# Values as the stationary operand in three attention mixers, two heads side by side in the columns of the array

## The chip, the cores and the metric

The kernel runs on one core of a Trainium2 chip. The metric is the device time of one execution in microseconds (us). The core's engines are TensorE (PE in the rows, and PEld for its weight loads), VectorE (DVE), ScalarE (ACT), GpSimd (POOL) and SyncE (SP), and DMA queues move data. PE works at one of two clocks, 1.2 or 2.4 GHz; the profile states the granted clock of a stretch as a share of 2.4 GHz.

## What is computed

Two stacks of two layers on 512 tokens of 1024 features, all in float32. A layer of block 1 mixes tokens in three ways (mLSTM, HGRN2, sliding-window attention with sinks) and then has an MLP and a gated embedding. A layer of block 2 mixes with differential, dilated and forgetting attention and then has a gated MLP with a convolution. The three attentions that the change touches, cut to what matters:

```python
# window attention (block 1): 8 query heads on 2 key/value heads of 64, window 128
m = jnp.maximum(jnp.max(s, axis=-1, keepdims=True), sink)
pexp = jnp.exp(s - m)
probs = pexp / (jnp.sum(pexp, axis=-1, keepdims=True) + jnp.exp(sink - m))
o = jnp.einsum('bnhgqk,bnkhd->bnqhgd', probs.astype(v.dtype), vv)

# forgetting attention (block 2): 6 heads of 64, causal
s = jnp.einsum('bhqd,bhkd->bhqk', qblk, k).astype(jnp.float32) * scale
s = s + fq[..., :, None] - cum_logf[..., None, :]
s = jnp.where(kpos[None, :] <= qpos[:, None], s, -jnp.inf)
p = jax.nn.softmax(s, axis=-1)
return jnp.einsum('bhqk,bhkd->bhqd', p, vf)

# dilated attention (block 2): 6 heads of 64, a mixture of windowed patterns,
# which the kernel computes as one softmax with an additive table c_dil
```

## The kernel before

**Numbers.** A large product is made of three (`mm3`, L176 to L178): each operand is split into a high and a low part (`split`, L136 on ACT and L137 on DVE), and high x high, high x low and low x high are summed in PSUM. These "triple products" are the projections. The attentions' own products (scores, transposes, product with the values) are plain float32, each of scores and values in two records.

**Tiles.** 512 tokens are four token tiles of 128 (`NT = 4`). Names of tiles: `ysw`, `yc`, `yb`, `ya` hold values and outputs by token (128 tokens in the partitions); `slotA` and `slotB` hold feature-major data; `wh` and `wl` are split weights, which `wload` brings ahead (`wr`, three buffers).

**PSUM.** `ps(tag)` takes a tile from one of four rings: "mm" with three buffers, "S" and "T" with two each, "o" with one. Buffers of a ring go round in the order of the program. Projections take "mm" (inside `held` also "S" and "T"), scores take "S", transposes "T", and the output of an attention tile is "o".

**Window attention** (`swa`). First a preparation: squares and sums of the heads (L534, L535), a reciprocal root (`rsqrt`, L121 to L132), the rotation (L548 to L559), and 20 transposes into feature-major queries and keys (L564). Then for each token tile and each of 8 heads: score (L581), masked maximum (L583, L584), exponential with its sum (L585), transposes (L590); after two heads a copy to `sw_pT` (L593) and the product with the values (L597), with the transposed probabilities as the stationary operand and 64 columns of values moving. At the end of a token tile all eight heads are scaled by the reciprocal sums in one DVE instruction (L603). Behind it in the program stand `feat(0)`, `feat(1)` and the `w_hi1` projection.

**Forgetting attention** (in `mixers2`, L1149 on). Gates: four transposes (L1136), steps on 6 x 512 (L1141 to L1147), a DMA to DRAM (`fg_d`) and, for each head and token tile, a DMA that broadcasts it to all partitions (`fg_b`, L1157, issued by POOL). Then `softmax_block` (score L1093, causal mask by a product L1096, DVE L1099, exponential L1100) and `pv` (transposes L1109, copy L1111, product with the values L1113). Token tiles go from the last to the first; L1162 scales. Behind it in the program stand the projections of differential attention (`w_a2`, through `rope_proj`; its steps L1068 to L1071, L1085, L1086).

**Dilated attention** (`attend`, L1219 on) is built in the same way with the table `c_dil`, token tiles 0 to 3, in two halves. After each half its output is transposed (L1251), split and projected (`w_ob2`); behind the first half stand also the projections `w_oa2`.

**Order.** Nothing here is ordered by hand. The program states the work mixer by mixer; a scheduler at build time moves instructions of later parts ahead where their operands and buffers are free by the program's own order of rings. So projections that stand behind a mixer can run between its steps. `tick` and `start` (L216 to L240) let the steps of the next normalization advance with the work of PE.

Of the kernel before, what the change touches and what calls it, by code (L numbers as in the profile page):

```python
# [9 lines left out]
F32 = mybir.dt.float32  # L10
F32R = mybir.dt.float32r
# [3 lines left out]
ALU = mybir.AluOpType  # L15
# [4 lines left out]
P = 128  # L20
S = 512
NT = S // P
# [39 lines left out]
class Builder:  # L62
# [328 lines left out]
    def mixers1(self, l, mp, act, nxt):  # L391
        nc = self.nc
        X, Y = self.sets
# [34 lines left out]
        ysw = [mp.tile([P, 768], F32, name=f"ysw{t}") for t in range(NT)]  # L428
# [16 lines left out]
        w = self.wload("w_hi1", l, 8 * 256)  # L445
# [8 lines left out]
        w = self.wload("w_mv1", l, 8 * 264, parts=4)  # L454
# [42 lines left out]
        sink = lambda m, pt, sl: nc.vector.tensor_tensor(self.x[m][:, sl], self.x[m][:, sl], pt, ALU.add)  # L497
        act = [self.to_feat(X, sub(ysw, i), "mm") for i in range(4)]
        for g in range(2):
# [23 lines left out]
    def swa(self, l, mp, sp, ysw, row):  # L523
# [44 lines left out]
        for t in range(NT):  # L568
# [9 lines left out]
            for j in range(8):  # L578
# [524 lines left out]
    def pv(self, mp, s, t, po, v):  # L1103
# [8 lines left out]
        for c in range(t + 1):  # L1112
            nc.tensor.matmul(po, pT[:, c * P:c * P + P], v(c), start=c == 0, stop=c == t)  # L1113

    def mixers2(self, l, mp, act, nxt):
        nc = self.nc
# [34 lines left out]
        for t in reversed(range(NT)):  # L1151
            po = self.ps("o")
            den = mp.tile([P, 6], F32, name="at_den", tag="at_den", bufs=2)
            for h in range(6):
                fbt = mp.tile([P, S], F32, name="fg_b", tag="fg_b", bufs=3)
                w = (t + 1) * P
                nc.gpsimd.dma_start(fbt[:, :w], fd[0, h * S:h * S + w].partition_broadcast(P))  # L1157
                b = (h % 2) * 64
                s, dn = self.softmax_block(mp, qk[h // 2][b:b + 64], qk[3 + h // 2][b:b + 64], t, fbt[:, :w], 0.125, True)
                nc.vector.reciprocal(den[:, h:h + 1], dn)  # L1160
                self.pv(mp, s, t, po[:, h * 64:h * 64 + 64], lambda c: yc[c][:, h * 64:h * 64 + 64])
            nc.vector.tensor_tensor(yc[t][:, 0:384].rearrange("p (h e) -> p h e", e=64),  # L1162
                                    po[:, 0:384].rearrange("p (h e) -> p h e", e=64),
                                    den.unsqueeze(2).broadcast_to([P, 6, 64]), ALU.mult)

# [50 lines left out]
        sub = lambda y, i: [y[t][:, i * P:i * P + P] for t in range(NT)]  # L1216
        act = [self.to_feat(X, sub(yc, i)) for i in range(3)] + [self.to_feat(X, sub(ya, i)) for i in range(2)]

        def attend(t):  # L1219
            po = self.ps("o")  # L1220
            den = mp.tile([P, 6], F32, name="at_den", tag="at_den", bufs=2)
            for h in range(6):
                b = (h % 2) * 64
                s, dn = self.softmax_block(mp, qkb[h // 2][b:b + 64], qkb[3 + h // 2][b:b + 64], t,
                                           self.c_dil[:, (3 - t) * P:], 0.125)
                nc.vector.reciprocal(den[:, h:h + 1], dn)
                self.pv(mp, s, t, po[:, h * 64:h * 64 + 64], lambda c: yb[c][:, h * 64:h * 64 + 64])
                self.tick(3000)
            nc.vector.tensor_tensor(yo[t].rearrange("p (h e) -> p h e", e=64),
                                    po[:, 0:384].rearrange("p (h e) -> p h e", e=64),  # L1230
                                    den.unsqueeze(2).broadcast_to([P, 6, 64]), ALU.mult)

# [6 lines left out]
        for sl in HALVES:  # L1239
# [3 lines left out]
            if wo is None:  # L1243
# [277 lines left out]
```

## Time and profile before

| | |
|---|---|
| median of 3 runs | 2808.39 us (2804.37 to 2814.62) |
| the profiled execution | 2820.27 us |
| its span | 2818.4 us |
| mean granted clock | 0.984 |
| PE busy | 2749.6 us, 98% |
| DVE, ACT, POOL busy | 63%, 42%, 8% |

The profiled execution stands 0.4% above the median. A row of the timeline gives the start, the busy time, engine, line and operation of consecutive equal instructions, then the tiles, partitions x elements, and a count; in brackets stands the idle time of the engine just before, with what ended it. Records of PE overlap each other, so what one costs is read from the distance between starts, not from its duration.

### The profile page before, as it was taken

To read this page: it belongs to the slowest core of one execution; us is meant where nothing else is said; L and a number is where in the kernel's file an instruction comes from. 1 tells how busy PE (TensorE), PEld (TensorE's weight loads), DVE (VectorE), ACT (ScalarE), POOL (GpSimd) and SP (SyncE) were. 2 spreads that over 40 slices of the span, in tenths; PEclk is the share of its full clock that TensorE was granted. 3 is DMA by queue.
4 is the path that set the end of the run, shared out by engine and by line. 5 is a ranking of instruction groups with operands and counts; after the bars stand their busy time and mean duration, and the time that the engine had idled before them with its cause. 6 is when DMAs were issued, how large, how long until landed. Compare 5 with 4: busy or idle time off the path is not lost.

```text
span 2818.4 us, 42688 instructions
## 1 busy us (share of the span) xinstructions
PE 2749.6 (98%) x16408; PEld 2350.0 (83%) x16408; DVE 1778.9 (63%) x3842; ACT 1176.3 (42%) x2296; POOL 214.2 (8%) x558
## 2 busy tenths in 40 slices
PE   8999999999999999999999999999999999999998
PEld 7887887889978788788987888888889787988887
DVE  7677777468767857756844656655554375665555
ACT  4644532236374553232634445433234444442332
POOL 2000100002200010000212100000000210000000
PEclk9998999999999999999999999999999999999999
DMA  4211486332221128733223121223332312133222
GB/s 153 75 50 50 141 266 222 105 103 92 85 70 46 61 93 265 254 120 105 91 75 111 31 70 64 84 88 96 100 106 77 87 36 86 39 105 98 90 88 77
DMA packets 87645, 285.61 MB, mean 101 GB/s; under 512 B 10972, under 2 KB 15132, under 8 KB 87440
## 3 DMA queue, kind: packets, MB, share of 16 engines
q1 hardware_dynamic: 81280, 266.49, 29.5%
q0 software_dynamic: 5872, 16.35, 2.3%
q8 instruction: 129, 2.11, 0.3%
q14 instruction: 76, 0.62, 0.1%
q10 hardware_dynamic: 288, 0.03, 0.0%
HBM read 280.69 MB, written 2.14 MB: 100 GB/s over the span
## 4 chain that ended last, share of the span: by engine, by line
PE 78%; DVE 8%; DMA 7%; ACT 2%; POOL 2%; issue 2%; SPq 0%; DVEq 0%; POOLq 0%; ACTq 0%
PE ps_mm L176 12%; PE ps_mm L177 12%; PE ps_mm L178 12%; DMA wm<-w_mod 6%; PE ps_T L176 5%; PE ps_T L177 5%; PE ps_T L178 5%; PE ps_S L176 5%; PE ps_S L177 5%; PE ps_S L178 5%; PE ps_S L1093 3%; PE ps_o L1113 2%; DVE wm L1032 2%; PE ps_T L1109 1%; PE ps_S L581 1%
## 5 line engine op out<-in xcount | busy, mean ns | idle before, releaser
L136 ACT CAST wh<-wr 128x1024 fp32r<-128x1024 f32 (+4 forms) x414 | 407.2, 986 | 672.5 <-PE ps_mm L177 209.3
L137 DVE TENSOR_TENSOR wl<-wr,wh 128x1024 fp32r<-128x1024 f32 (+4 forms) x414 | 476.0, 1151 | 317.4 <-ACT wh L136 309.9
L177 PE MATMUL ps_mm<-slotA,wh 128*128 128x512 f32 (+1 forms) x632 | 229.0, 364 | 3.4 <-DVE slotA L317 2.0
L176 PE MATMUL ps_mm<-slotA,wh 128*128 128x512 f32 (+1 forms) x632 | 226.5, 365 | 1.5 <-ACT slotA L316 0.7
L178 PE MATMUL ps_mm<-slotA,wl 128*128 128x512 f32 (+1 forms) x632 | 226.3, 360 | 0.0
L176 PE MATMUL ps_mm<-wh,slotA 128*128 128x256 f32 (+3 forms) x688 | 208.7, 304 | 1.3 <-DVE rp_b L1070 1.3
L178 PE MATMUL ps_mm<-wh,slotA 128*128 128x256 f32 (+3 forms) x688 | 206.1, 300 | 0.0
L177 PE MATMUL ps_mm<-wl,slotA 128*128 128x256 f32 (+3 forms) x688 | 205.7, 299 | 0.0
L1032 DVE CUSTOM_DVE_ANT_0 wm<-wm,sc 128x1024 f32<-128x1024 f32 x96 | 117.5, 1224 | 65.9 <-DMA wm<-w_mod 65.2
L136 ACT CAST m_h<-tmp 128x512 fp32r<-128x512 f32 (+1 forms) x122 | 71.4, 587 | 207.6 <-DVE tmp L911 171.3
L176 PE MATMUL ps_mm<-slotB,wh 128*128 128x512 f32 (+1 forms) x408 | 141.9, 357 | 2.6 <-ACT slotB L136 1.6
L177 PE MATMUL ps_mm<-slotB,wh 128*128 128x512 f32 (+1 forms) x408 | 142.5, 351 | 1.4 <-DVE slotB L137 1.4
L176 PEld LDWEIGHTS ps_mm<-wh,slotA 128*128 128x128 f32 x688 | 131.4, 191 | 13.7 <-issue 12.2
L177 PEld LDWEIGHTS ps_mm<-slotA,wh 128*128 128x128 f32 x632 | 122.3, 194 | 22.7 <-issue 3.1
L178 PE MATMUL ps_mm<-slotB,wl 128*128 128x512 f32 (+1 forms) x408 | 140.7, 346 | 0.0
L176 PEld LDWEIGHTS ps_mm<-slotA,wh 128*128 128x128 f32 x632 | 121.4, 194 | 22.7 <-issue 3.6
L178 PEld LDWEIGHTS ps_mm<-slotA,wl 128*128 128x128 f32 x632 | 122.3, 193 | 17.5 <-issue 2.6
L178 PEld LDWEIGHTS ps_mm<-wh,slotA 128*128 128x128 f32 x688 | 131.4, 191 | 6.2 <-issue 5.1
L177 PEld LDWEIGHTS ps_mm<-wl,slotA 128*128 128x128 f32 x688 | 131.5, 191 | 5.8 <-issue 5.0
L176 PE MATMUL ps_S<-m_h,wh 128*128 128x512 f32 (+1 forms) x355 | 129.5, 365 | 2.4 <-DVE yacc L945 2.1
L1100 ACT ACTIVATE at_s<-at_s,at_st 128x512 f32<-128x512 f32 (+3 forms) x160 | 89.6, 560 | 98.3 <-DVE at_st L1099 91.2
L178 PE MATMUL ps_S<-m_h,wl 128*128 128x512 f32 (+1 forms) x355 | 129.3, 364 | 0.0
(631 smaller groups left out, 7289.9 us busy)
## 6 DMA issues: line engine op xcount, KB each, us to landing
wr<-w_up SPq DMA_DIRECT2D x152, 512.0 KB, 3.8
wm<-w_mod SPq DMA_DIRECT2D x96, 512.0 KB, 4.6
wr<-w_dn SPq DMA_DIRECT2D x64, 512.0 KB, 3.9
wr<-w_dn SPq DMA_DIRECT2D x32, 384.0 KB, 3.0
wr<-w_dn SPq DMA_DIRECT2D x32, 320.0 KB, 2.8
wr<-w_f SPq DMA_DIRECT2D x16, 512.0 KB, 3.8
wr<-w_pg SPq DMA_DIRECT2D x16, 512.0 KB, 3.8
wr<-w_t SPq DMA_DIRECT2D x12, 512.0 KB, 4.7
```

The lines of the kernel that those rows point to most:

```text
L136: nc.scalar.copy(hi, src)
L137: nc.vector.tensor_tensor(lo, src, hi.bitcast(F32), ALU.subtract)
L176: nc.tensor.matmul(out, ah, bh, start=i == 0, stop=False)
L177: nc.tensor.matmul(out, ah, bl, start=False, stop=False)
L178: nc.tensor.matmul(out, al, bh, start=False, stop=i == n - 1)
L581: nc.tensor.matmul(pt, qs[f][b:b + 64, tt], qs[4][b:b + 64, k0:k0 + w], start=True, stop=True)
L1032: nc.vector.tensor_tensor_reduce(w, w, self.sc, 1.0, 0.0, ALU.mult, ALU.add, accum_out=self.mod[l][:, j:j + 1])
L1093: nc.tensor.matmul(pt, q[:, t * P:w], k[:, 0:w], start=True, stop=not tri, tile_position=None if row is None else (row, 0))
L1100: nc.scalar.activation(s, s, AF.Exp, bias=st[:, 0:1], scale=-1.0, accum_out=st[:, 1:2])
L1109: nc.tensor.transpose(tp[:, c * P:c * P + P], s[:, c * P:c * P + P], self.ident)
L1113: nc.tensor.matmul(po, pT[:, c * P:c * P + P], v(c), start=c == 0, stop=c == t)
```

## The change

In the three mixers the product with the values is turned round. The values (128 tokens x 64 features of one head) are the stationary operand, the transposed probabilities (128 queries) move, and two heads go to the two column halves of the array by `tile_position` (0,0) and (0,64). The output has features in the partitions: two heads in 128 rows, queries along the columns. To scale it, `out_scaled` needs the reciprocal sums in the same layout: POOL spreads them over 64 columns a head, PE transposes them into a PSUM tile of the ring "mm", ACT copies them, and DVE multiplies. Outputs are now feature-major, so `to_feat` and the transposes at the end of dilated attention give way to `parts_of` and plain splits. In forgetting and dilated attention two heads now go together through `pv2`. Differential attention keeps `pv`.

```diff
-        act = [self.to_feat(X, sub(ysw, i), "mm") for i in range(4)]
+        act = [self.parts_of(X, ysw, i) for i in range(4)]
...
-                    for jj in (j - 1, j):
-                        for c in range(w // P):
-                            o, v = (jj % 2) * w + c * P, 640 + (jj % 2) * 64
-                            nc.tensor.matmul(po[:, jj * 64:jj * 64 + 64], pT[:, o:o + P], ysw[k0 // P + c][:, v:v + 64],
-                                             start=c == 0, stop=c == w // P - 1)
+                    for c in range(w // P):
+                        for u in range(2):
+                            o, v = u * w + c * P, 640 + u * 64
+                            nc.tensor.matmul(po[u * 64:u * 64 + 64, f * P:f * P + P], ysw[k0 // P + c][:, v:v + 64],
+                                             pT[:, o:o + P], start=c == 0, stop=c == w // P - 1, tile_position=(0, u * 64))
...
-            nc.vector.tensor_tensor(ysw[t][:, 0:512].rearrange("p (h e) -> p h e", e=64),
-                                    po.rearrange("p (h e) -> p h e", e=64),
-                                    den.unsqueeze(2).broadcast_to([P, 8, 64]), ALU.mult)
+            self.out_scaled(ysw[t][:, 0:512], po, den, 4)
...
+    def pv2(self, mp, ss, t, po, v):
...
+        w = (t + 1) * P
+        pTs = []
+        for s in ss:
+            tp = self.ps("T")
+            for c in range(t + 1):
+                nc.tensor.transpose(tp[:, c * P:c * P + P], s[:, c * P:c * P + P], self.ident)
+            pT = mp.tile([P, S], F32, name="at_pT", tag="at_pT", bufs=3)[:, :w]
+            nc.scalar.copy(pT, tp[:, :w])
+            pTs.append(pT)
+        for c in range(t + 1):
+            for u, pT in enumerate(pTs):
+                nc.tensor.matmul(po[u * 64:u * 64 + 64], v(c, u), pT[:, c * P:c * P + P], start=c == 0, stop=c == t,
+                                 tile_position=(0, u * 64))
+
+    def out_scaled(self, dst, po, rden, n):
...
+        pr = self.ps("mm")
+        rb = self.tmp()[:, 0:n * P]
+        nc.gpsimd.tensor_copy(rb.rearrange("p (h e) -> p h e", e=64), rden.unsqueeze(2).broadcast_to([P, 2 * n, 64]))
+        for i in range(n):
+            nc.tensor.transpose(pr[:, i * P:i * P + P], rb[:, i * P:i * P + P], self.ident)
+        nc.scalar.copy(rb, pr[:, 0:n * P])
+        nc.vector.tensor_tensor(dst, po[:, 0:n * P], rb, ALU.mult)
+
+    def parts_of(self, which, ys, i):
...
+        h, lo = self.slot(which, F32R), self.slot(which, F32R)
+        for t in range(NT):
+            tt = slice(t * P, t * P + P)
+            self.split(h[:, tt], lo[:, tt], ys[t][:, i * P:i * P + P])
+        return h, lo
...
-            for h in range(6):
...
-                nc.vector.reciprocal(den[:, h:h + 1], dn)
-                self.pv(mp, s, t, po[:, h * 64:h * 64 + 64], lambda c: yb[c][:, h * 64:h * 64 + 64])
-                self.tick(3000)
...
+            for i in range(3):
...
+                self.pv2(mp, ss, t, po[:, i * P:i * P + P], lambda c, u: yb[c][:, (2 * i + u) * 64:(2 * i + u) * 64 + 64])
+                self.tick(6000)
+            self.out_scaled(yo[t], po, den, 3)
...
-            for i in range(3):
-                pt = self.ps("T")[:, 0:S // 2]
-                for u, t in enumerate(ts):
-                    nc.tensor.transpose(pt[:, u * P:u * P + P], yo[t][:, i * P:i * P + P], self.ident)
-                self.split(aa[i][0][:, sl], aa[i][1][:, sl], pt)
+            for t in ts:
+                tt = slice(t * P, t * P + P)
+                for i in range(3):
+                    self.split(aa[i][0][:, tt], aa[i][1][:, tt], yo[t][:, i * P:i * P + P])
```

The order of instructions moves with it. First PE in window attention of the first layer, where its first token tile ends and the second begins, before the change. L176 to L178 are triple products, L581 scores, L590 transposes, L597 products with the values:

```order
L177 MATMUL ps_mm_1612<-wl_1551,slotA_114 128x264
L597 MATMUL ps_o_770<-ysw0_205,sw_pT_824 128x64 x2
L581 MATMUL ps_S_879<-sw_q4_765,slotB_744 128x256
L178 MATMUL ps_mm_1612<-wh_1550,slotA_115 128x264
L590 MATMUL ps_T_862<-ident_81,sw_s_858 128x128 x2
L176 MATMUL ps_mm_1612<-wh_1550,slotA_116 128x264
L581 MATMUL ps_S_888<-sw_q4_765,slotB_744 128x256
L177 MATMUL ps_mm_1612<-wl_1551,slotA_116 128x264
L178 MATMUL ps_mm_1612<-wh_1550,slotA_117 128x264
L176 MATMUL ps_mm_1640<-wh_1532,slotA_102 128x264
L177 MATMUL ps_mm_1640<-wl_1533,slotA_102 128x264
L597 MATMUL ps_o_770<-ysw0_205,sw_pT_843 128x64 x2
```

The same engine and place after the change; L1137 are the transposes of `out_scaled`:

```order
L581 MATMUL ps_S_864<-sw_q4_765,slotB_737 128x256
L597 MATMUL ps_o_770<-sw_pT_805,ysw0_205 64x128 x2
L581 MATMUL ps_S_873<-sw_q4_765,slotB_737 128x256
L590 MATMUL ps_T_834<-ident_81,sw_s_830 128x128
L597 MATMUL ps_o_770<-sw_pT_824,ysw0_205 64x128 x2
L590 MATMUL ps_T_834<-ident_81,sw_s_838 128x128
L581 MATMUL ps_S_887<-sw_q4_765,slotB_744 128x256
L590 MATMUL ps_T_870<-ident_81,sw_s_866 128x128 x2
L581 MATMUL ps_S_896<-sw_q4_765,slotB_744 128x256
L597 MATMUL ps_o_770<-sw_pT_843,ysw0_205 64x128 x2
L1137 MATMUL ps_mm_851<-ident_81,tmp_852 128x128 x4
L590 MATMUL ps_T_870<-ident_81,sw_s_875 128x128 x2
```

Between the steps of the attention stood triple products of the projections before; now the steps follow each other without any.

The second place is PE at the end of forgetting attention in the first layer of block 2, before the change. L1109 are transposes, L1113 products with the values, L1093 and L1096 score and mask:

```order
L177 MATMUL ps_mm_15444<-wl_15383,slotA_13680 128x256
L178 MATMUL ps_mm_15444<-wh_15382,slotA_13681 128x256
L176 MATMUL ps_mm_15444<-wh_15382,slotA_13682 128x256
L177 MATMUL ps_mm_15444<-wl_15383,slotA_13682 128x256
L1113 MATMUL ps_o_14878<-yc0_14482,at_pT_14961 128x64
L1113 MATMUL ps_o_14878<-yc1_14483,at_pT_14961 128x64
L1109 MATMUL ps_T_14995<-ident_81,at_s_14990 128x128
L1093 MATMUL ps_S_15032<-slotB_14067,slotB_14064 128x128
L1096 LDWEIGHTS identb_14052
L1096 MATMUL ps_S_15032<-trib_14054,identb_14052 128x128
L1093 MATMUL ps_S_15047<-slotB_14068,slotB_14065 128x128
L1113 MATMUL ps_o_14878<-yc0_14482,at_pT_14978 128x64
```

And after it, where L1121 are the transposes of `pv2` and L1127 its products with the values:

```order
L1127 MATMUL ps_o_15076<-at_pT_15100,yc0_14554 64x128
L1127 MATMUL ps_o_15076<-at_pT_15104,yc0_14554 64x128
L1127 MATMUL ps_o_15076<-at_pT_15130,yc0_14554 64x128
L1121 MATMUL ps_T_15158<-ident_81,at_s_15143 128x128
L1127 MATMUL ps_o_15076<-at_pT_15134,yc0_14554 64x128
L1127 MATMUL ps_o_15076<-at_pT_15160,yc0_14554 64x128
L1121 MATMUL ps_T_15162<-ident_81,at_s_15153 128x128
L1127 MATMUL ps_o_15076<-at_pT_15164,yc0_14554 64x128
L1137 MATMUL ps_mm_15168<-ident_81,tmp_15169 128x128 x3
L176 MATMUL ps_mm_15192<-wh_15182,slotA_13752 128x256
L177 MATMUL ps_mm_15192<-wl_15183,slotA_13752 128x256
L178 MATMUL ps_mm_15192<-wh_15182,slotA_13753 128x256
```

The first triple product of the projections for differential attention, on `ps_mm_15192`, now stands behind the last transposes of `out_scaled` (L1137); before, triple products stood between the steps.

## Rows read from the trace of the kernel before

**Rows 1.** The page, part 1: busy us, share of the span, instructions.

```profile
PE 2749.6 (98%) x16408; PEld 2350.0 (83%) x16408; DVE 1778.9 (63%) x3842; ACT 1176.3 (42%) x2296; POOL 214.2 (8%) x558
```

**Rows 2.** The page, part 4: the chain that ended last, by engine.

```profile
PE 78%; DVE 8%; DMA 7%; ACT 2%; POOL 2%; issue 2%; SPq 0%; DVEq 0%; POOLq 0%; ACTq 0%
```

**Rows 3.** Windows: from:to, length, busy us of engines, granted clock, DMA share, GB/s.

```profile
78.30:166.50 88.20, 88.20 (x554) 70.67 (x552) 52.22 (x170) 50.77 (x117) 1.07 (x2) 1.00 0.22 70
...
1505.60:1572.00 66.40, 65.99 (x439) 52.60 (x440) 25.23 (x94) 33.03 (x86) 14.21 (x25) 0.95 0.30 74
...
1507.50:1514.20 6.70, 6.70 (x22) 4.63 (x23) 2.29 (x10) 4.17 (x10) 2.35 (x4) 0.51 0.51 142
1705.50:1712.10 6.60, 6.60 (x20) 3.79 (x19) 1.98 (x8) 2.10 (x7) 0.00 (x0) 0.51 0.06 25
...
1514.40:1572.00 57.60, 57.60 (x414) 47.38 (x414) 21.93 (x79) 27.82 (x74) 11.31 (x20) 1.00 0.27 64
```

**Rows 4.** Timeline of PE at 2.4 GHz in forgetting attention.

```profile
1515.77 1.12 PE L1093 MATMUL ps_S<-slotB 64*128 64x512 f32 x2
1516.83 2.00 PE L1113 MATMUL ps_o<-yc,at_pT 128*128 128x64 f32 x16
1518.66 1.04 PE L1109 MATMUL ps_T<-ident,at_s 128*128 128x128 f32 x8
1519.54 0.22 PE L1096 MATMUL ps_S<-trib,identb 128*128 128x128 bf16 x1
```

**Rows 5.** Timeline of PE: scores between triple products of 256 columns, window attention.

```profile
85.81 0.28 PE L176 MATMUL ps_mm<-wh,slotA 128*128 128x256 f32 x1
85.93 0.28 PE L177 MATMUL ps_mm<-wl,slotA 128*128 128x256 f32 x1
86.14 0.48 PE L581 MATMUL ps_S<-sw_q,sw_q 64*128 64x128 f32 x2
86.55 0.39 PE L178 MATMUL ps_mm<-wh,slotA 128*128 128x256 f32 x1
86.77 0.28 PE L176 MATMUL ps_mm<-wh,slotA 128*128 128x256 f32 x1
```

**Rows 6.** Timeline of PE: records of one 64x64 tile.

```profile
871.53 1.14 PE L729 MATMUL ps_S<-tmp 64*64 64x64 f32 x16
872.61 0.44 PE L590 MATMUL ps_T<-ident,sw_s 128*128 128x128 f32 x2
```

**Rows 7.** Timeline of PE: records that alternate between two column halves.

```profile
911.15 1.91 PE L733 MATMUL ps_S<-tmp 64*64 64x64 f32 x64
912.99 0.39 PE L177 MATMUL ps_mm<-wl,slotB 128*128 128x256 f32 x1
```

**Rows 8.** Timeline of PE: the first steps of forgetting attention.

```profile
1505.71 1.12 PE L1093 MATMUL ps_S<-slotB 64*128 64x512 f32 x2 [2.73 <-DVE at_st L1099]
...
1507.30 2.07 PE L1093 MATMUL ps_S<-slotB 64*128 64x512 f32 x2 [0.29 <-DVE at_st L1099]
...
1509.38 1.92 PE L1109 MATMUL ps_T<-ident,at_s 128*128 128x128 f32 x8
```

**Rows 9.** Groups of PE in 78.3:166.5: busy us, mean ns, then idle before.

```profile
L176 PE MATMUL ps_mm<-wh,slotA 128*128 128x256 f32 (+1 forms) x69 | 20.4, 301 | 0.0
...
L176 PE MATMUL ps_mm<-slotA,wh 128*128 128x512 f32 x32 | 13.5, 423 | 0.0
```

**Rows 10.** The same groups in 1505.6:1572.

```profile
L176 PE MATMUL ps_mm<-wh,slotA 128*128 128x256 f32 x61 | 18.4, 301 | 0.0
```

**Rows 11.** Timeline of DVE: preparation of window attention, second layer.

```profile
761.14 0.48 DVE L406 SCALAR_TENSOR_TENSOR ysw<-ps_mm,rt,brow 128x256 f32<-128x256 f32 x1
...
774.29 0.33 DVE L559 TENSOR_TENSOR ysw<-sw_a,sw_b 128x160 f32<-128x160 f32 x1
```

**Rows 12.** Pieces of the chain of waits through the gates: start us, us, what.

```profile
1489.39 0.74 DVE fg_f L1141
...
1500.13 6.39 DMA fg_b<-fg_d
```

More of the change, by code (lines that the diff above doesn't have):

```diff
@@ L1113, in pv @@
             nc.tensor.matmul(po, pT[:, c * P:c * P + P], v(c), start=c == 0, stop=c == t)
+    def pv2(self, mp, ss, t, po, v):
+        nc = self.nc
+        w = (t + 1) * P
[12 more added lines that the diff above has]
+    def out_scaled(self, dst, po, rden, n):
+        nc = self.nc
+        pr = self.ps("mm")
[11 more added lines that the diff above has]
+        return h, lo
     def mixers2(self, l, mp, act, nxt):
@@ L1153, in mixers2 @@
             den = mp.tile([P, 6], F32, name="at_den", tag="at_den", bufs=2)
-            for h in range(6):
[L1155 to L1159, printed above, removed]
-                nc.vector.reciprocal(den[:, h:h + 1], dn)
[L1161 to L1164, printed above, removed]
+            for i in range(3):
+                ss = []
+                for h in (2 * i, 2 * i + 1):
+                    fbt = mp.tile([P, S], F32, name="fg_b", tag="fg_b", bufs=3)
+                    w = (t + 1) * P
+                    nc.gpsimd.dma_start(fbt[:, :w], fd[0, h * S:h * S + w].partition_broadcast(P))
+                    b = (h % 2) * 64
+                    s, dn = self.softmax_block(mp, qk[i][b:b + 64], qk[3 + i][b:b + 64], t, fbt[:, :w], 0.125, True)
+                    nc.vector.reciprocal(den[:, h:h + 1], dn)
+                    ss.append(s)
+                self.pv2(mp, ss, t, po[:, i * P:i * P + P], lambda c, u: yc[c][:, (2 * i + u) * 64:(2 * i + u) * 64 + 64])
+            self.out_scaled(yc[t][:, 0:384], po, den, 3)
         qka = [self.slot(Y) for m in range(4)]
@@ L1216, in mixers2 @@
         sub = lambda y, i: [y[t][:, i * P:i * P + P] for t in range(NT)]
-        act = [self.to_feat(X, sub(yc, i)) for i in range(3)] + [self.to_feat(X, sub(ya, i)) for i in range(2)]
+        act = [self.parts_of(X, yc, i) for i in range(3)] + [self.to_feat(X, sub(ya, i)) for i in range(2)]
         def attend(t):
@@ L1221, in attend @@
             den = mp.tile([P, 6], F32, name="at_den", tag="at_den", bufs=2)
[L1222 to L1226, printed above, removed]
-                self.pv(mp, s, t, po[:, h * 64:h * 64 + 64], lambda c: yb[c][:, h * 64:h * 64 + 64])
-                self.tick(3000)
-            nc.vector.tensor_tensor(yo[t].rearrange("p (h e) -> p h e", e=64),
-                                    po[:, 0:384].rearrange("p (h e) -> p h e", e=64),
-                                    den.unsqueeze(2).broadcast_to([P, 6, 64]), ALU.mult)
+            for i in range(3):
+                ss = []
+                for h in (2 * i, 2 * i + 1):
+                    b = (h % 2) * 64
+                    s, dn = self.softmax_block(mp, qkb[i][b:b + 64], qkb[3 + i][b:b + 64], t,
+                                               self.c_dil[:, (3 - t) * P:], 0.125)
+                    nc.vector.reciprocal(den[:, h:h + 1], dn)
+                    ss.append(s)
+                self.pv2(mp, ss, t, po[:, i * P:i * P + P], lambda c, u: yb[c][:, (2 * i + u) * 64:(2 * i + u) * 64 + 64])
+                self.tick(6000)
+            self.out_scaled(yo[t], po, den, 3)
         yo = [self.slot(X)[:, 0:384] for t in range(NT)]
@@ L1247, in mixers2 @@
                 aa = [(self.slot(Y, F32R), self.slot(Y, F32R)) for _ in range(3)]
-            for i in range(3):
-                pt = self.ps("T")[:, 0:S // 2]
-                for u, t in enumerate(ts):
-                    nc.tensor.transpose(pt[:, u * P:u * P + P], yo[t][:, i * P:i * P + P], self.ident)
-                self.split(aa[i][0][:, sl], aa[i][1][:, sl], pt)
+            for t in ts:
+                tt = slice(t * P, t * P + P)
+                for i in range(3):
+                    self.split(aa[i][0][:, tt], aa[i][1][:, tt], yo[t][:, i * P:i * P + P])
             self.feat_group(wo, 3, 8, aa, sink, 0, (sl,))
```

## The prediction

> **What bounds the kernel now.** I read the busy times first: TensorE (PE) works for 98% of the span [rows 1]. The chain of waits agrees: 78% of it lies on PE [rows 2]. So the question for every edit is what it does to PE's own stream, and then whether PE keeps being fed. Next I read the stretches in which the three mixers run, by the table of windows [rows 3]. In the window-attention stretch (78.3 to 166.5) PE is busy for 88.20 of 88.20 us at a granted clock of 1.00, that is 2.4 GHz. In the forgetting stretch (1505.6 to 1572) it is busy for 65.99 of 66.40 us. It is full there because projections run between the attention steps: 207 triple-product records of 256 or 264 columns and 96 of 512 in the first [rows 9], some 181 in the second [rows 10]. Attention alone is a chain from PE through DVE and ACT and back to PE; the projections are its cover.
>
> **Step 1, the product with the values.** Per layer 56 matmuls change in window attention, 60 in forgetting and 60 in dilated attention. Each makes two records, and there are two layers: 704 records. Sixteen of them start 1516.83 and the next row starts 1518.66 [rows 4]: .114 us a record, 80 us in all. The new matmul streams 128 columns, for which the nearest row is the transpose, eight in .88 us [rows 4], .110 each. Two heads sit in the two column halves. Where the kernel already uses column halves, 64 records take 1.84 us [rows 7], 29 ns each, against 16 in 1.08 us, 67 ns, for records of the same size in a single tile [rows 6]: halves overlap. So 704 x .110 / 2 = 39 us, a gain of 41 us; if the halves ran one after the other, 77 us and a gain of 3. I take the first, by rows 6 and 7. On the same point the Trainium skill ("TensorEngine Tiling (Array Packing)", Performance Considerations) recommends this very swap for a moving size up to 64, with a gain of up to two.
>
> **Step 2, the changes of array shape.** PE now goes from the whole array to column halves and back. In the order of instructions the shape changes 640 times instead of 475, 165 more. A visit of two score records between triple products costs [rows 5]: from 85.93 to 86.77 is .84 us, less two products at .12 (85.81 to 85.93) and two records of 128 columns at .11 leaves .38 for two changes, .19 each. 165 x .17 to .19 = 28 to 31 us. Against this change speaks a rule of the Trainium skill (same page, Key Properties): a change of tiling mode drains the engine. The rows agree, with .19. Steps 1 and 2 leave a gain of some 12 us. The 80 transposes that `out_scaled` adds are as many as those no longer made by `to_feat` and the dilated end: nothing.
>
> **Step 3, what the order does.** `out_scaled` takes its PSUM tile from "mm", once per token tile, in program order; no mixer step took from that ring of three before. The projections that stand behind the mixer in the program need the same ring. The order shows the result: in all of window attention, its preparation included, and in all of forgetting attention no projection is left between the steps; they stand behind the last `out_scaled`. The work of the projections is not lost, it comes later; but the stretches have no cover. Four prices per layer:
>
> Preparation of window attention. From the last L406 to the last L559 DVE needs from 761.14 to 774.6 [rows 11], of which three or four weight splits of 1.2 us are other work: about 9 us, then 20 transposes with copies between. PE worked on projections there. I take +10 us (6 to 14).
>
> Gates of forgetting attention. From L1141 at 1489.39 to the end of the DMA that broadcasts fg_b at 1506.5 [rows 12] is 17 us, some 1.5 of it other DVE and POOL work. PE sat idle for only 2.73 [rows 8] and about another 1 of this; the rest were projections. I take +12 us (8 to 14).
>
> The two attention stretches themselves. Without cover PE's own work is, at full clock: window attention 24 scores at .43, 8 at .21, 72 transposes at .11, 28 pairs at .22 and 72 changes at .17 = 38 us. Before, the stretch held 88.2 - 207 x .12 - 96 x .23 - 2 of other products = 39 us of attention. Forgetting: 6 scores each of .85, .64, .43 and .21, 24 masks at about .1 (an estimate from the transposes), 72 transposes, 30 pairs and 85 changes = 44 us, where before there were 66.4 - 181 x .12 - 1 = 44. So at full clock only waits are added, 5 and 8 us by my estimate: the score, two DVE steps, the exponential, the transposes and a copy follow one another, with two score tiles in flight.
>
> The clock decides the rest. Behind 2.73 us of idle the first two score records of 512 columns still took 1.12 us, the next two 2.07 and eight transposes 1.92 [rows 8], against 1.12 and 1.04 at full clock [rows 4]: PE had gone to 1.2 GHz, granted clock .51, and stayed there though it was busy without a break [rows 3]; full clock is back at 1514.4, after a body of triple products. The second cold place, 1705.5 to 1712.1, has PE busy for all of 6.60 us with scores and a few transposes, also at .51 [rows 3]. Each place in this profile in which attention steps run without a body of projections shows this. After the change both stretches begin with 10 us or more of idle and no triple product comes until they end. So I take 1.2 GHz for all of them: 1.9 x 38 = 72 and 1.9 x 44 = 84, that is +33 and +40 us a layer.
>
> Dilated attention. Its first two token tiles lose their cover as well: 6 scores at .21 and 6 at .43, 24 transposes, 9 pairs and 23 changes, some 12 us at full clock and 23 at half: +11. The last two tiles ran mostly bare before. The saved columns less the changes of shape give -2 there.
>
> **Step 4, the ends.** After each half of dilated attention the output projection waits for POOL's spreading of the reciprocals, three transposes, a copy, a multiplication and six splits, where a multiplication, transposes and three splits stood: about +2 for each half, +4 a layer (0 to 8). POOL's steps stand behind the broadcast DMAs on its queue; those for the next tile are issued early, so I count no more. Later in block 1 the two other mixers lose attention work as a cover of their own chains: 0 to 10 a layer, not in the sum.
>
> **The sum.** Per layer: 10 + 12 + 33 + 40 + 11 - 2 + 4 = 108, for two layers of each block 216 us. The profiled execution took 2820.3, so 3036; it stands 0.4% above the median of 2808.4, so 3024 against the median.
>
> **Rivals.** (a) The clock stays at 2.4 GHz, or comes back soon after each start, since PE works steadily enough with scores and transposes. For it: mixed stretches show 1.00 throughout. Against it: both cold places stayed cold while PE was full. Then per layer 10 + 12 + 4 + 8 + 4 - 2 + 4 = 40, in all 80: 2900, or 2889 against the median. Between it and the forecast lie mixtures, in which one of the two stretches warms up.
> (b) The other side, not slower. Cover doesn't matter, because the projections only move: DVE and ACT, relieved of the weight splits in the stretch, run ahead of PE, the preparation overlaps with other work, and what remains is steps 1 and 2, -12 us: 2797, -0.4%. It decides if idle before the first scores stays below 1 to 2 us a stretch. Against it is the order: behind L559 and behind the gates there is no PE work that could run.
> (c) The change doesn't do what it says: the column halves don't overlap. Then +38 at full clock, more at half: 3070 with the forecast's clock, 2930 with (a).
> (d) A change of shape costs more into and out of column halves than into and out of the row halves of [rows 5]: with .4 instead of .19 the 165 added changes cost 66 us instead of 31, +35. No row shows it, and it only adds.
>
> **How the numbers follow.** Forecast (half clock in the bare stretches) 0.6; (a) with its mixtures 0.28; (c) and (d) 0.07; (b) 0.05. The predicted time is that of the first. The range reaches from (a) at 2889 up to the forecast with the upper bounds of preparation, gates, ends and later chains (+4, +2, +4, half of 10, twice: +30) and a part of (c): 3075. What is left out is (b), most of (c), and (a) at its best. A measurement of this kernel can tell about 0.5% from no change. Faster by more than that needs (b) and a better step 1: 0.02. Within 0.5%, (b): 0.03. Slower: 0.95.
>
> **What would show it.** In the profile after, PE's busy share should fall by few points while PEclk shows 5 or 6 in the slices that hold the mixers; the rows of the new products should start about .055 us apart at full clock; there should be idle of some 10 us before the first L564 or L581 and of 15 before the first score with fg_b; no triple product should stand between scores. The forecast is wrong if the granted clock in these stretches is 1.00, if new product records start .11 apart at full clock, or if triple products stand among them.

## The result: 2934.8 us, 4.4% slower

The changed kernel takes 2934.78 us (median of 4 runs, 2917.99 to 2949.98) against 2809.89 for the kernel before in the same series: a ratio of 1.044, 95% interval 1.041 to 1.047. The forecast was 3024 us with a range of 2885 to 3075, and slower at 0.95. Sign and main cause came out as forecast; the size lies between the forecast and its rival (a). The profiled execution of the changed kernel is the fastest of the four, 2917.99 us (span 2916.2), and that of the kernel before, 2820.27, is slower than all four of its timed runs; so the two traces differ by 98 us where the medians differ by 125.

Parts 1 and 2 of the page after; the second line is the granted clock in 40 slices of the span:

```profile
PE 2793.7 (96%) x16408; PEld 2334.4 (80%) x16408; DVE 1782.0 (61%) x3896; ACT 1195.2 (41%) x2374; POOL 230.9 (8%) x582
...
PEclk8699999999989999999997999999999998999999
```

PE's share falls from 98% [rows 1] to 96% while its busy time rises by 44 us: idle and half clock both grew. The windows after, by stretch (length, then busy us of PE, PEld, DVE, ACT, POOL, granted clock): window attention of the first layer from its first score on, two pieces of it in the second layer, then in forgetting attention the wait for the gates and two pieces of the stretch:

```profile
68.40:131.00 62.60, 61.80 (x216) 32.53 (x218) 22.06 (x106) 29.60 (x81) 1.84 (x3) 0.50 0.00 1
802.00:831.00 29.00, 28.52 (x98) 15.20 (x100) 11.10 (x57) 13.67 (x43) 0.61 (x1) 0.50 0.00 1
831.00:853.00 22.00, 20.75 (x150) 12.46 (x146) 11.84 (x61) 16.39 (x45) 1.87 (x3) 1.00 0.00 1
1529.40:1545.50 16.10, 0.00 (x1) 0.04 (x1) 5.71 (x9) 5.08 (x6) 2.22 (x4) 0.54 0.41 138
1545.50:1561.50 16.00, 16.00 (x46) 7.46 (x46) 4.27 (x16) 6.77 (x16) 3.72 (x7) 0.51 0.29 86
1561.50:1595.70 34.20, 32.71 (x215) 19.45 (x214) 11.57 (x57) 18.75 (x59) 9.58 (x18) 1.00 0.30 53
```

Set beside [rows 3], where the same stretches stood at 1.00 and 0.95 with projections in them, this shows three things. PE does nothing for 16.1 us behind the first two scores of forgetting attention: the third waits for a buffer of the ring "S" until DVE (L1097) has added the broadcast gates (`fg_b`) to the first. The bare stretches begin at 1.2 GHz. And they don't stay there: full clock is back at 831 and at 1561.5 with no triple product having run. Only the first layer's window attention is at half clock nearly to its end. The timeline of PE after has the idle times (in brackets) and one group of the new products:

```profile
60.65 0.69 PE L564 MATMUL ps_T<-ident,ysw 128*128 128x128 f32 x2 [8.00 <-DVE ysw L559]
...
839.17 1.09 PE L597 MATMUL ps_o<-sw_pT,ysw 128*64 128x128 f32 x16
840.19 0.70 PE L581 MATMUL ps_S<-sw_q,slotA 64*128 64x256 f32 x2
...
1545.50 2.04 PE L1091 MATMUL ps_S<-slotB 64*128 64x512 f32 x2 [16.13 <-DVE at_st L1097]
```

Sixteen new records from 839.17 to 840.19 take 1.02 us, of which about .1 is the change of shape behind them: .057 each, against .114 in [rows 4].

Read along the program, by the same DVE and ACT instructions in both traces, the delay grows as follows: 26 us by the end of the first layer of block 1, 43 by the end of the second, 68 by the end of the first layer of block 2, 98 at the end.

### The profile page after: what moved, and what is told of

Read it like the earlier page. It is cut to its first block, busy times and chain, and to the rows that moved or that the text cites. A ratio compares the mean times of both kernels' runs of the same rounds, so it can differ in the third digit from the quotient of the medians.

```text
span 2916.2 us, 42907 instructions
## 1 busy us (share of the span) xinstructions
PE 2793.7 (96%) x16408; PEld 2334.4 (80%) x16408; DVE 1782.0 (61%) x3896; ACT 1195.2 (41%) x2374; POOL 230.9 (8%) x582
## 5 line engine op out<-in xcount | busy, mean ns | idle before, releaser
L176 PE MATMUL ps_mm<-slotA,wh 128*128 128x512 f32 (+1 forms) x632 | 224.4, 360 | 1.7 <-ACT slotA L316 0.9
L178 PE MATMUL ps_mm<-slotA,wl 128*128 128x512 f32 (+1 forms) x632 | 224.1, 356 | 0.0
L176 PE MATMUL ps_mm<-wh,slotA 128*128 128x256 f32 (+3 forms) x688 | 206.6, 301 | 6.1 <-DVE rp_b L1068 4.5
L178 PE MATMUL ps_mm<-wh,slotA 128*128 128x256 f32 (+3 forms) x688 | 204.6, 298 | 0.0
L1091 PE MATMUL ps_S<-slotB 64*128 64x512 f32 (+7 forms) x320 | 117.8, 539 | 33.2 <-DVE at_st L1097 33.2
L176 PE MATMUL ps_mm<-slotB,wh 128*128 128x512 f32 (+1 forms) x408 | 141.0, 350 | 4.1 <-ACT slotB L136 3.9
L176 PEld LDWEIGHTS ps_mm<-wh,slotA 128*128 128x128 f32 x688 | 131.9, 192 | 14.5 <-issue 11.2
L178 PE MATMUL ps_mm<-slotB,wl 128*128 128x512 f32 (+1 forms) x408 | 140.5, 346 | 0.0
L178 PEld LDWEIGHTS ps_mm<-wh,slotA 128*128 128x128 f32 x688 | 131.7, 191 | 6.7 <-issue 6.3
L176 PEld LDWEIGHTS ps_mm<-slotA,wh 128*128 128x128 f32 x632 | 120.3, 192 | 20.9 <-issue 2.4
L178 PEld LDWEIGHTS ps_mm<-slotA,wl 128*128 128x128 f32 x632 | 121.6, 192 | 16.0
L176 PE MATMUL ps_S<-m_h,wh 128*128 128x512 f32 (+1 forms) x355 | 129.7, 365 | 2.1 <-DVE yacc L943 1.8
L178 PE MATMUL ps_S<-m_h,wl 128*128 128x512 f32 (+1 forms) x355 | 129.4, 365 | 0.0
```

The lines of the kernel that those rows point to most:

```text
L176: nc.tensor.matmul(out, ah, bh, start=i == 0, stop=False)
L178: nc.tensor.matmul(out, al, bh, start=False, stop=i == n - 1)
L1091: nc.tensor.matmul(pt, q[:, t * P:w], k[:, 0:w], start=True, stop=not tri, tile_position=None if row is None else (row, 0))
```

## The experiments

**Theory.** `out_scaled` takes a tile of the ring "mm" in each token tile; that keeps the projections out of the mixers, and idle time and half clock follow. **Rival.** The new layout itself costs: changes of shape, heads in pairs, a longer chain at each token tile. The first runs change the ring alone, in either kernel.

### The PSUM tile from another ring (e1_ring_t, e1_ring_s)

```diff
     def out_scaled(self, dst, po, rden, n):
-        pr = self.ps("mm")
+        pr = self.ps("T")      # e1_ring_s: "S"
```

> The changed kernel with one word altered: out_scaled takes its PSUM tile from the ring of the transposes (T) and not from that of the projections (mm). In the order, triple products stand between the attention steps again (263 records in each window-attention stretch, 196 in each forgetting stretch). Theory (the ring mm took the cover away): idle before the first scores and the cold clock go, steps 1 and 2 of the prediction are what is left, some 12 us below before: about 2797 us, ratio 0.990 to 1.002. Rival (the new layout itself costs: changes of array shape, the longer chain of out_scaled, heads in pairs): still above 2850, ratio above 1.015.

> The same with the ring of the scores (S). The order holds more triple products in the stretches (414 and 271). Theory: as with T, 2785 to 2815, ratio 0.990 to 1.002; if scores have to wait for out_scaled's tile it is up to 1% above the other. Rival: above 2850.

Measured with T: 2877.68 us, ratio 1.023 (1.021 to 1.026). With S: 2900.77, ratio 1.031 (1.029 to 1.033). By the number the rival came out (above 2850), but its cause, the new layout, did not, as the run with neither ring will show. The ring "mm" accounts for about half of the loss, and something else for 64 us. The windows of the T run: the stretch behind window attention, and the two places where its clock is low longest:

```profile
160.00:214.00 54.00, 54.00 (x514) 48.07 (x514) 52.13 (x124) 36.57 (x65) 3.71 (x7) 1.00 0.22 69
224.00:275.00 51.00, 43.08 (x300) 33.84 (x301) 26.32 (x48) 21.42 (x50) 2.42 (x4) 0.50 0.07 22
947.00:1026.00 79.00, 65.18 (x431) 52.56 (x432) 48.09 (x121) 30.81 (x71) 5.82 (x10) 0.50 0.07 21
```

Attention is covered again. But from 160 to 214 DVE is busy for 52 of 54 us, and the recurrences of HGRN2 and mLSTM behind it run at half clock with PE idle for 8 and 14 us. The first instruction of HGRN2's gates on DVE is L635 before (L633 in the changed file). Here it is in the trace of before, with the step L419 that makes its operand, and then in that of the T run:

```profile
66.72 0.69 DVE L419 TENSOR_TENSOR slotB<-ps_mm,R 128x512 f32<-128x512 f32 x1
...
70.61 0.68 DVE L635 SCALAR_TENSOR_TENSOR tmp<-slotB 128x512 f32<-128x512 f32 x1
```

```profile
65.42 0.68 DVE L419 TENSOR_TENSOR slotB<-ps_mm,R 128x512 f32<-128x512 f32 x1
...
160.57 0.64 DVE L633 SCALAR_TENSOR_TENSOR tmp<-slotB 128x512 f32<-128x512 f32 x1
```

Its operand is there at the same time, yet it starts 90 us later: it writes a `tmp` tile, and `out_scaled` takes one of the four `tmp` buffers per token tile, ahead of it in the order of the program. So a second shared ring was a new theory. With S, 23 us more, the clock was low for 217 us of the execution, with T for 184.

### Each ring alone, in the kernel before (e2_before_ring, e7_before_tmp, e8_before_mm)

These keep the old layout and only take tiles: at the end of each token tile of the three mixers one more transpose and a copy that nobody reads.

```diff
+    def ring_take(self, y):
+        nc = self.nc
+        pr = self.ps("mm")                      # e7: "T"
+        nc.tensor.transpose(pr[:, 0:P], y[:, 0:P], self.ident)
+        rb = self.tmp()[:, 0:P]                 # e8: a tile of its own
+        nc.scalar.copy(rb, pr[:, 0:P])
...
+            self.ring_take(ysw[t])              # likewise yc[t], yo[t]
```

> The kernel before, in which each token tile of the three mixers ends with one more transpose into a tile of the ring mm and a copy of it that nobody reads; the layout of the product with the values is the old one. In the order no triple product is left in the two stretches. Theory: the loss comes from the ring alone, so this shows all of it without the gain of steps 1 and 2: 2920 to 2960 us, ratio 1.035 to 1.055. Rival (layout): 2812 to 2820, ratio 1.00 to 1.004.

> The same in the kernel before with the extra transpose in ring mm and the copy in a tile of its own: only the ring of the projections is taken. Theory: nearly all of the run with both rings (3049), since the gates of HGRN2 need the projections that now come late in any case: 3020 to 3050, ratio 1.073 to 1.085. Rival (the two rings add up): 2985 to 3005, ratio 1.062 to 1.068.

> The kernel before with one extra transpose per token tile of the three mixers into ring T and a copy into tmp: only the ring tmp is taken, projections keep their ring, the layout is the old one. Theory: HGRN2's gates wait for window attention, some +50 us as in block 1 of the T run: 2850 to 2870, ratio 1.014 to 1.025. Rival: 2812 to 2820, ratio 1.00 to 1.004.

Measured: both rings 3049.15 us, ratio 1.083 (1.081 to 1.086); "mm" alone 3043.89, 1.083 (1.080 to 1.087); `tmp` alone 2898.30, 1.033 (1.030 to 1.035). So 24 transposes in all, a few us of work, cost 236 us by the place of their tiles. The ring is the cause without any new layout, and more than the changed kernel shows; I had expected at most 2960 us with both rings. `tmp` alone costs more than I expected, and adds nothing where "mm" is taken: HGRN2's gates need projections that come late then anyway. In the trace with "mm" alone the first L419 starts at 152.2 us and the gates at 154.2, in the changed kernel at 141.2 and 143.2. Windows of the run with "mm" alone, in window attention and in forgetting attention:

```profile
66.00:149.00 83.00, 80.79 (x259) 54.49 (x258) 24.25 (x117) 33.08 (x92) 0.00 (x0) 0.50 0.00 1
1590.00:1670.00 80.00, 73.78 (x255) 49.32 (x256) 17.92 (x76) 25.99 (x76) 12.90 (x24) 0.50 0.22 50
```

With the old layout these bare stretches, which all begin after idle time, stay at 1.2 GHz throughout. They are the stretches that the prediction priced for the changed kernel.

### Neither ring (e5_no_shared_ring)

```diff
-        pr = self.ps("mm")
-        rb = self.tmp()[:, 0:n * P]
+        pr = self.ps("T")
+        rb = rb[:, 0:n * P]     # handed in: a tile of sw_pT or at_pT
```

> As the run with out_scaled's PSUM tile in ring T, and its SBUF tile taken from the mixers' own rings (sw_pT, at_pT) and no longer from tmp, the ring that the gates of HGRN2 (L635 on) use next. In the trace of the T run those gates began at 160.6 us where they began at 70.6 before, though their operand was there at 66, and the recurrences behind them ran bare at half clock. Theory (the ring tmp is the second culprit): the gates start near 70 again, the excess of block 1 in the T run (+17.6 and +32 us) goes, block 2 keeps its +6: 2805 to 2835 us, ratio 0.997 to 1.008. Rival (tmp is innocent, the new layout costs): no change from the T run, 2870 to 2885, ratio 1.02 to 1.026.

Measured: 2825.73 us, ratio 1.006 (1.004 to 1.008). As the theory said: of the 125 us, 18 are left when `out_scaled` takes its tiles from the mixers' own rings. What is left is the new layout with its cover back. In its trace the gates start at 70.6 again. In the order, shape changes number 669 against 475 before. A low clock remains in the recurrences of block 1:

```profile
60.00:160.00 100.00, 99.41 (x617) 77.88 (x616) 59.93 (x188) 58.09 (x121) 2.93 (x5) 1.00 0.22 69
245.00:276.00 31.00, 30.22 (x115) 25.15 (x116) 18.87 (x62) 14.24 (x39) 3.63 (x6) 0.51 0.06 19
962.00:986.00 24.00, 23.36 (x83) 18.48 (x83) 12.02 (x45) 8.11 (x20) 1.30 (x3) 0.51 0.03 9
```

In the order the output projection of window attention (`w_oa1`) is used up before the last 40 products of mLSTM (L868), among which it stood before. The trace agrees so far that no triple product runs there from 237.0 to 274.4 us and from 943.4 to 983.6, where before the longest such piece was 12.6 us. That the early use of `w_oa1` is the reason is argued from the order; no run isolates it.

### Window attention as before, block 2 in the new layout (e10_block2_only)

```diff
-            self.out_scaled(ysw[t][:, 0:512], po, den, 4, sp.tile([P, S], F32, name="sw_pT", tag="sw_pT", bufs=2))
+            nc.vector.tensor_tensor(ysw[t][:, 0:512].rearrange("p (h e) -> p h e", e=64),
+                                    po.rearrange("p (h e) -> p h e", e=64),
+                                    den.unsqueeze(2).broadcast_to([P, 8, 64]), ALU.mult)
...
-        act = [self.parts_of(X, ysw, i) for i in range(4)]
+        act = [self.to_feat(X, sub(ysw, i), "mm") for i in range(4)]
```

> The run without shared rings, with window attention put back to its old form: only forgetting and dilated attention have the new layout, with out_scaled in the rings T and at_pT. In the trace of that run block 1 was 6.9 us longer than before and block 2 4.8 us shorter. Theory (saved columns and changes of shape nearly cancel, and what window attention still cost is the early use of w_oa1 as cover): 2797 to 2808 us, ratio 0.996 to 1.001. Rival (the new layout costs in block 2 as well, and the profile's 4.8 us were chance): 2812 to 2822, ratio 1.002 to 1.006.

Measured: 2812.16 us against 2806.96, ratio 1.002 (1.000 to 1.003). That is the lower edge of the rival's range, and no gain. Along the program the delay against before changes by only -0.7 us over block 2 in the two traces. So in block 2 the halved columns just about pay for the changes of shape, and the 4.8 us that the earlier trace seemed to win were chance. Most of the 0.6% of the run without shared rings thus belongs to window attention; the long low pieces in the recurrences of block 1 are gone in this trace (3.4 us each at 211.4 and 914.6). The same two traces show how far single traces can be trusted: block 1 has the same code in both, and yet it is 11.9 us shorter in this one, where the clock was low for 43 us of the whole execution against 91 in the trace of before.

### Columns one after the other (e11_serial_halves, e12_after_serial)

```diff
-        for c in range(t + 1):
-            for u, pT in enumerate(pTs):
+        for u, pT in enumerate(pTs):
+            for c in range(t + 1):
```

and likewise in window attention. e11 starts from the run without shared rings, e12 from the changed kernel.

> The run without shared rings, with the products of one head all ahead of those of the other, so that neighbouring records mostly use the same column half. Theory (two halves overlap, .055 us a record against .11): up to 704 x .055 = 39 us more than the run without shared rings, less where a record of one head still meets the other's: 2850 to 2868 us, ratio 1.015 to 1.021. Rival (halves don't overlap, the records of a pair only start together): no change, 2820 to 2832, ratio 1.004 to 1.009.

Measured: 2847.11 us, ratio 1.015 (1.012 to 1.017), 21 us above the run without shared rings and just below what was expected. Sixteen records in the paired order, then in the serial order, each with the row behind it:

```profile
1527.37 1.09 PE L1127 MATMUL ps_o<-at_pT,yc 128*64 128x128 f32 x16
1528.39 0.87 PE L1121 MATMUL ps_T<-ident,at_s 128*128 128x128 f32 x6
```

```profile
1525.89 1.58 PE L1127 MATMUL ps_o<-at_pT,yc 128*64 128x128 f32 x16
1527.40 0.77 PE L1121 MATMUL ps_T<-ident,at_s 128*128 128x128 f32 x5
```

1.02 us against 1.51: halves overlap where neighbours lie in different halves. The serial group is still a mixture: neighbours in the same half start .109 to .110 us apart, and where records of both halves meet, two start in that time. By the starts the serial order costs 14 us in forgetting and dilated attention; the two traces stand 29 us apart, and in that of e11 the clock was low for 32 us more, worth about 16 (an estimate: half of them). So the 21 us need not be the halves alone. In window attention the order changed nothing (17 us for all its new records in both traces): its heads have one or two blocks, and records of the two halves still meet (6 to 14 ns apart in the serial order).

> The changed kernel as it is (shared rings, bare stretches) with the products of one head ahead of those of the other. In the kernel before with the ring mm taken (3044 us) the bare stretches stayed at half clock for 92 to 96 us each; in the changed kernel full clock came back after 75, 41, 31 and 27 us. Theory A (records in pairs make the attention steps dense enough on PE for full clock to come back): without the pairs the stretches stay at half clock longer, 2990 to 3050 us, ratio 1.065 to 1.087. Theory B (the changed layout brings full clock back in either order, and only the 21 us of the serial halves are added, some more where they run at half clock): 2950 to 2975, ratio 1.05 to 1.06.

Measured: 2943.09 us, ratio 1.044 (1.039 to 1.050). Neither theory: it is the changed kernel's own time within the scatter. In its trace the half clock in forgetting attention lasts 31 us a layer, as in the changed kernel (31 and 27), and in window attention 85 and 79 against 75 and 41. So the pairs are not what brings full clock back in forgetting attention. For window attention nothing can be said: in the runs with the idle time filled, which keep the pairs, it stood at half clock for 20 to 82 us a layer. What in the new layout brings full clock back, against the old one in the run with "mm" taken, stays open.

### The idle time filled (e4_filled_idle, e9_filled_idle_2)

```diff
+    def filler(self, y, n):
+        pt = self.ps("S")
+        for i in range(n):
+            nc.tensor.matmul(pt[:, 0:w], y[:, 0:P], y, start=i == 0, stop=i == n - 1)
+        nc.scalar.copy(self.tmp()[:, 0:1], pt[:, 0:1])      # not in e9
...
+        self.filler(ysw[3][:, 640:768], 36)      # before swa
...
+        self.filler(yc[3][:, 0:384], 22)         # before the token tiles of forgetting attention
```

> The changed kernel with useless work of PE in the idle time: 36 matmuls of 128 columns (7.7 us) before the first transposes of window attention and 22 of 384 columns (14 us) before the first scores of forgetting attention; results are not used. The stretches themselves stay without projections. Half-clock theory: the stretches start at 2.4 GHz and the idle time is spent in any case, so what goes is the half clock in them: 63 us at half clock in the first layer, some 29 in the second, 16 in each forgetting stretch make 124 us, half of it saved if the clock stays up: about 2870, ratio 1.015 to 1.03. Rival (the idle time is the whole loss, or the bare attention steps fall to 1.2 GHz by themselves): no change from after, 2920 to 2945, ratio 1.04 to 1.05.

> The changed kernel with useless PE work in the idle time as in the run before it, without the copy of its result: that copy had stood ahead of the squares of window attention on ACT and held them back by 8 us, so window attention still began after idle time. Half-clock theory: what begins at 2.4 GHz stays there, in window attention as it did in forgetting attention (which showed no half clock with the filler): 63 and 29 us at half clock in window attention and 16 in each forgetting stretch, half of it saved: 2870 to 2885, ratio 1.02 to 1.026. Rival (window attention falls to 1.2 GHz by itself): only forgetting's 16 us go: 2910 to 2925, ratio 1.035 to 1.04.

Measured: 2930.34 us, ratio 1.041 (1.037 to 1.044), and 2924.27, ratio 1.040 (1.036 to 1.044): no change that can be told from the changed kernel. The first had a flaw of mine: the copy of the result stood ahead of the squares on ACT, and the first transposes came 10 us late (70.6 us against 60.7). The second answers the question in two parts. Forgetting attention in it, from the filler's last 5 us on (it ends at 1533.4):

```profile
1528.00:1580.00 52.00, 50.53 (x281) 27.86 (x279) 16.60 (x76) 25.78 (x75) 15.53 (x29) 0.97 0.34 77
```

It begins at 2.4 GHz and stays there until 1577.0, 4 us before projections return, bare as it is. Window attention of the first layer, from the end of the filler on:

```profile
60.30:68.00 7.70, 5.12 (x34) 3.35 (x32) 2.70 (x15) 5.23 (x11) 0.00 (x0) 1.00 0.00 0
68.00:88.00 20.00, 19.81 (x67) 10.20 (x67) 7.39 (x38) 10.29 (x32) 0.61 (x1) 0.51 0.00 1
88.00:130.00 42.00, 40.75 (x246) 28.40 (x246) 19.10 (x77) 25.12 (x60) 4.68 (x9) 0.99 0.05 14
```

It begins at 2.4 GHz, PE is busy for 5.1 of the next 7.7 us, with short waits between transposes and first scores, and falls to 1.2 GHz by itself; here it recovers after 20 us, in the second layer only after 65. So half clock is not the idle time's doing alone: window attention, with the short waits of its start, makes its own, forgetting attention doesn't. By the delay along the program the first layer of block 1 won 21 us against the changed kernel, the second lost 15, and the forgetting stretches won 7 and 6. That is lost again by the end of each layer of block 2, where the delay grows by 13 and 12 us instead of 0 and 3: the first tiles of dilated attention stood at half clock for 27 us in each layer, against 14 and 17. Why they did, no run shows.

## Why the prediction was right where it was, and where it missed

**The order and the ring (step 3).** Right, and shown: with the ring alone taken, the old layout loses 236 us; with neither ring taken, the new one loses 18. What step 3 did not see is the second ring. It counted PSUM only and overlooked that `tmp` is handed out in program order as well; of the 64 us that the T run left, this made some 46. In the changed kernel it hardly shows, since "mm" holds back the same work.

**Column halves (step 1).** Right for records that meet: .057 us a record after, .110 / 2 forecast. But not all of them meet. In the trace without shared rings 264 of the 704 new records start within 8 ns of the one before, which makes 264 pairs and leaves 176 records without a partner; most of these stand in 53 visits in which one product, two records of one head, comes alone. The records without their changes of shape thus take 48 us (an estimate: 264 pairs and 176 single records at .109 to .110 each), not 39, and before they took 75, not 80: a gain of 27 us where 41 were forecast.

**Changes of shape (step 2).** About right in total, by two errors that cancel. With the cover restored there are 194 more changes, not 165, since projections stand between again, and each is cheaper: by the starts in the trace without shared rings a visit to the column halves costs .09 us behind it, .05 among its first records and .09 at the record ahead of it, .23 for two changes where .34 to .38 were forecast. At 121 visits that is 28 us at most; 28 to 31 were forecast. The 704 records with the change of shape behind them need 66 us against 75 before; the change ahead of them takes up to 11 more. So nothing is left of the 12 us that were forecast for steps 1 and 2, and e10 measures the same in block 2. No run came near rival (b)'s 2797.

**Idle time (step 3, preparation and gates).** Right: 8.0 us before the first transposes and some 2 more before the scores (10 forecast), and 16.1 before the first score that waits for a step with fg_b, where 12 more than the former 4 were forecast.

**Half clock (step 3, "so I take 1.2 GHz for all of them").** This is the term that was mis-sized. Forecast: 72 us for window attention and 84 for forgetting attention, in each layer. Measured: window attention from 68.4 to 135.7 (67 us) in the first layer, and 51 in the second; forgetting attention 50 from 1545.5 to 1595.7, with 16 us at half clock. That is 34 us less in each forgetting stretch. The reasoning from two short cold places of [rows 3], that a bare stretch stays cold until triple products come, failed for the new layout: full clock came back in the middle of scores, transposes and products with values. For the old layout it held in stretches that begin after idle time, as the run with "mm" taken shows (3044 us, the four long stretches at .50). Its premise, that every place of attention steps without projections is cold, was wrong in the trace of before already. The last tiles of dilated attention ran there without any triple product, with only a few products of the next normalization (L259, L266) or the transposes L1251 among their steps, and at 2.4 GHz:

```profile
1723.20:1735.40 12.20, 11.68 (x89) 9.19 (x88) 6.77 (x22) 8.36 (x22) 3.25 (x16) 1.00 0.02 4
...
2411.30:2428.60 17.30, 15.60 (x122) 12.68 (x120) 11.88 (x35) 12.38 (x31) 3.25 (x16) 1.00 0.01 4
```

Both begin at 2.4 GHz, directly behind triple products. And the second cold place is not bare, as step 3 read it: 12 of its 20 PE records are triple products. So the trace of before held evidence for rival (a) that the prediction did not weigh. Whether the long stretches of the old layout would stay at 2.4 GHz if they began there, no run shows.

**Dilated attention and the ends (+11, -2, +4).** Too high. Along the program the delay grows by 25 and 30 us over the two layers of block 2, of which forgetting attention with its gates makes 24 and 26; 1 and 4 are left where 13 were forecast.

**The sum.** 216 us were forecast, and 98 came in the trace (125 by the medians). By the delay along the program the 118 that are missing lie in block 1 with 43 (26 and 17 came, 43 a layer were forecast), in forgetting attention and its gates with 54 (24 and 26 against 52), and in dilated attention and the ends with 21 (1 and 4 against 13). These shares are those of two single traces. With e10's trace in place of that of before, block 1 would have lost 12 us more.

## What to carry to other kernels

Before a step is added inside a stretch that is covered by later work, look at every ring its tiles come from, in PSUM and in SBUF: a buffer taken in program order holds back all later users of that ring, and the cost is that of their cover, not of the step. Compare the order of instructions before and after for the work that used to stand between; here the halved columns saved some 27 us before the changes of shape, and the tags of two tiles lost some 106. And a layout that changes the array's shape for two to sixteen records at a time should be charged for each change: here they ate the whole gain.

## What the runs showed of the hardware

A stretch of bare attention steps (no triple products among them) may run at either clock: forgetting attention in the new layout held 2.4 GHz for 44 us behind the filler, when it began there, dilated attention in the old one for 12 and 17 us, and forgetting attention came back to it from 1.2 after 16 us (31 with the idle time before); the same steps in the old layout, begun after idle time, stayed at 1.2 GHz for 92 us a stretch (granted clock .50). Window attention in the new layout, behind the filler, fell from 2.4 to 1.2 GHz after 8 us in which PE was busy for two thirds, and recovered after 20 us in one layer and 65 in the other. The four timed executions of the changed kernel differ by 1.1%, with mean granted clocks from .946 to .958 that follow their times. At 2.4 GHz two records in different column halves start 6 to 7 ns apart, and the next pair .109 to .110 us behind the start of the first; records in the same half start .109 to .110 us apart each.
